# Far-score work placed by the length of VectorE's queue, and fewer small VectorE operations, in a hybrid decoder layer

## The chip, the cores and the metric

One Trainium2 chip, one of its cores. The metric is the device time of one execution in microseconds (us), the median of several runs. TensorE multiplies matrices (PE in the profile, its weight loads PEld), VectorE (DVE), ScalarE (ACT) and GpSimd (POOL) work element by element, and SyncE (SP) issues nearly all DMAs from one queue.

## What is computed

One layer for a prompt of 512 tokens and for 8 samples of 4 tokens each, 544 rows in all, in fp32. Between two gated feed-forward blocks stands a mixer: one input projection feeds dilated attention (8 heads of 64) and an mLSTM (4 heads of 128), side by side, and an output projection joins them.

```python
x = x + 0.5 * swiglu(rmsnorm(x), ffn1)
z = rmsnorm(x) @ w_in
# attention, per head: softmax over windows (128, 1), (512, 4), (2048, 16) of (window, dilation),
# the three merged by their softmax denominators; samples read a cache of 2048 keys and values
m = max(s); p = exp(s - m); den = sum(p); o = (p / den) @ v
# mLSTM, per head, in chunks of 128 tokens
d = where(causal, b[t] - b[s] + ig[s], -inf)
a = exp(d - m_t) * (q @ k.T)
num = a @ v + w_inter * (q @ C)
den = max(abs(sum(a) + w_inter * (q @ n)), exp(-m_t))
h = num / den
x = x + concat(attention, rmsnorm(h) * sigmoid(o_gate)) @ w_out
x = x + 0.5 * swiglu(rmsnorm(x), ffn2)
```

## The kernel before, in words

The activations lie transposed, 128 features by 544 rows to a tile. Every large product is made of three passes with operands split into a high and a low part (`whi`, `wlo` for weights; `xh`, `xl`, `mh`, `ml` and others for activations). ScalarE casts the high part and VectorE subtracts to get the low part (`Job.split`, L531). A job is one block of 128 output columns: 48 matmuls of 272 columns into the PSUM tile `mm` for a depth of 1024. The jobs run in a fixed order: feed-forward 1; the input projection (q, keys and values of the attention, then for each of the four mLSTM heads k, v, q and the output gate); the output projection in two passes (`wo`, L1780: first three mLSTM heads, then the four attention parts and the last mLSTM head); feed-forward 2.

The order of all other work is written while the program is built. The class `Order` (L54) keeps a modelled clock for each engine (`od.clock`) and a time `od.t` that goes with TensorE. The parts of the mixer are generators. Each yields the modelled time from which it wants to go on, and between the matmuls of the jobs `poll` (L100) lets every generator go on whose time has come. What it issues then takes the next place in its engine's queue. On the chip the queues are in order: an instruction that waits holds up what stands behind it on its engine.

The generators that the change touches:

- `far_scores` (L1136): for 8 samples and 6 blocks of cached keys, 48 times, it loads a key tile `kv` (and for each sample a broadcast query tile `qb`) by DMA, multiplies them on GpSimd into `pr` (128x512), and sums `pr` over 64 columns on VectorE into a slice of `big["sF"]`, which the profile calls `cb`, the tile that holds it. A product was placed when GpSimd's modelled clock was at most 1.5 us ahead, a sum when VectorE's was (`SCORE_AHEAD`, L45, L1163, L1168).
- `attn_pair` (L1350): prompt attention of two heads for one block of 128 queries. VectorE adds the mask to the scores and takes the row maxima `smax` (128x1 each, together 128x2), multiplies them by -0.125 (L1364), ScalarE takes the exponential with them as its bias, VectorE takes the reciprocal of the sums `sden`, ScalarE scales, TensorE transposes `pS` into `pT` and multiplies by the values. This runs 16 times.
- `ml_head` (L1590): one mLSTM head. VectorE adds a column of `cols` and the causal mask (part of the tile `ca`) to the row `E`, chunk by chunk; ScalarE exponentiates `E` whole; VectorE multiplies it with the products of q and k into `aT` (and `aTs` for the samples). `post` (L1649) forms the denominators `dn` with three small operations and a reciprocal, three times a head. GpSimd makes `qw`, `qm`, copies of the state's normaliser, and products with `hN` and `hf`.

The consumers of the far scores are `sample_soft` (L1410) and `sample_att` (L1455), for two groups of four samples. A group starts when its far scores are complete. Then 28 value tiles of the cache (`kv` from `cache_v_win`) are loaded and multiplied by TensorE; the second group's loads follow the last far score. The result feeds the second pass of the output projection. `reload` (L485) brings the eight tiles `x` back from DRAM for `wo`, by the same SP queue, and `E`, `W` and the state tiles `C` of each mLSTM head are loaded by it too.

Of the kernel before, what the change touches and what calls it, by code (L numbers as in the profile page):

```python
# [41 lines left out]
HB = B // 2  # L42
KS = float(P) ** -0.5
NT2 = 62
SCORE_AHEAD = 1.5  # L45
SCORE_PRIO = 1
SWITCH = 0.093
SLACK = 0.8
# [5 lines left out]
class Order:  # L54
# [89 lines left out]
    def R(self, *aps):  # L144
        return max(self.ready.get(a.tensor.name, (0.0, ""))[0] for a in aps) + 0.2
# [103 lines left out]
def hybrid_layer_kernel(ctx: ExitStack, tc: tile.TileContext, I: dict, C: dict, O: list):  # L249
# [23 lines left out]
    def bc(ap, axis, n):  # L273
        a = ap.unsqueeze(axis)
        shape = list(a.shape)
        shape[axis] = n
        return a.broadcast_to(shape)
# [858 lines left out]
    def far_scores():  # L1136
# [22 lines left out]
        for n, (b, i) in enumerate(order):  # L1159
            if n + 2 < len(order):  # L1160
                yield from fetch(*order[n + 2])
            k, q = ks[(b, i)], qs[b]
            yield max(R(k, q) - 0.3, od.clock["pool"] - SCORE_AHEAD)  # L1163
            pr = t2("pr", (P, ROW))
            pool.tensor_tensor(pr, k, q, op=OP.mult)
            pend.append((b, i, pr))
            if len(pend) > 1:
                yield max(R(pend[0][2]) - 0.3, od.clock["dve"] - SCORE_AHEAD)  # L1168
                reduce(*pend.pop(0))
            if n + 1 == len(order) // 2:  # L1170
                yield R(pend[0][2]) - 0.3
                reduce(*pend.pop(0))
                ev.add(("far", 0))
# [176 lines left out]
    def attn_pair(j, po, qbs):  # L1350
        for qb in qbs:
# [9 lines left out]
            for e, p in enumerate(ps2):  # L1361
                dve.tensor_tensor_reduce(out=s2[e][:, 0:w], in0=p[:, 0:w], in1=big["maskA"][:, (3 - qb) * P:], scale=1.0,
                                         scalar=-3.0e38, op0=OP.add, op1=OP.max, accum_out=mx[:, e:e + 1])
            dve.tensor_scalar(mx, mx, -0.125, None, op0=OP.mult)  # L1364
            done(*ps2)
            yield R(mx) - 0.4
            for e in range(2):
                act.activation(s2[e][:, 0:w], s2[e][:, 0:w], AF.Exp, bias=mx[:, e:e + 1], scale=0.125,
                               accum_out=dn[:, e:e + 1])
# [220 lines left out]
    def ml_head(h):  # L1590
# [7 lines left out]
            dma.dma_start(c0[:, :, 0:P], I["state_C"][i * HB:(i + 1) * HB, h].rearrange("b k v -> k b v"))  # L1598
        yield R(E, W) - 0.3, 0, lambda: "kws" in d and "vs" in d
        q, k, kw, kws, vm, vs, vb = (d[x] for x in ("q", "k", "kw", "kws", "vm", "vs", "vb"))  # L1600
        for c in range(CH):
            s_ = slice(c * P, (c + 1) * P)
            dve.scalar_tensor_tensor(E[:, s_], E[:, s_], cols[:, c, 0, h:h + 1], big["caus"], op0=OP.add, op1=OP.add)
        dve.scalar_tensor_tensor(E[0:NS, S:N], E[0:NS, S:N], cols[0:NS, CH, 0, h:h + 1], causS, op0=OP.add, op1=OP.add)
        qw = t2("qw")
        pool.tensor_tensor(qw, q, W, op=OP.mult)
        for i, c0 in enumerate(C0):
            pool.tensor_copy(c0[:, :, P], n0[:, i * HB:(i + 1) * HB, h])
        yield R(E) - 0.3
        act.activation(E[:, 0:S], E[:, 0:S], AF.Exp)  # L1610
        act.activation(E[0:NS, S:N], E[0:NS, S:N], AF.Exp)
        yield R(E) - 0.8, 2
        p, p2 = aux(), aux()
        for c in range(CH):
# [34 lines left out]
        def post(c0, nch, p, n, out):  # L1649
            dn, sq = small("dn", (P, 2), 4), small("sqj", (P, P), 2)  # L1650
            r = dn[0:n, 0:nch]
            dd = p[0:n, 0:nch * V1].rearrange("p (e v) -> p e v", v=V1)[:, :, P]
            dve.tensor_scalar(r, dd, -1.0, None, op0=OP.mult)
            dve.tensor_tensor(r, r, dd, op=OP.max)
            dve.tensor_tensor(r, r, cols[0:n, c0:c0 + nch, 2, h], op=OP.max)
            dve.reciprocal(r, r)
            yield R(dn) - 0.3
            for e in range(nch):
                act.activation(out(c0 + e), p[0:n, e * V1:e * V1 + P], AF.Copy, scale=dn[0:n, e:e + 1])
            done(p)  # L1660
            yield R(out(c0 + nch - 1)) - 0.3
            for e in range(nch):
                act.activation(sq[0:n], out(c0 + e), AF.Square, accum_out=ss[0:n, c0 + e:c0 + e + 1])
            posted.append(c0)
# [268 lines left out]
```

## Time and profile before

| | |
|---|---|
| time, three runs | 1125.67 us median (1123.56 to 1129.19) |
| the profiled execution's own time | 1125.39 us |
| its span, first to last instruction | 1123.2 us |
| TensorE busy | 1100.7 us (98%) |
| VectorE busy | 768.5 us (68%), 1228 instructions |
| ScalarE busy | 507.8 us (45%) |
| GpSimd busy | 92.5 us (8%) |
| granted TensorE clock, mean | 0.998 |
| HBM read, written | 132.57 MB, 9.18 MB |

The mixer runs from about 400 to 710 us of the span. GpSimd works in little else: its 48 products `pr` start between 475.3 and 595.5 us. Busy TensorE means that some matmul is in flight; matmuls overlap, so a busy share of 98% is not a rate of 98%.

### The profile page before, as it was taken

How to read it: one execution, taken by the hardware profiler on the slowest of the kernel's cores; microseconds unless marked ns; L12 is line 12 of the kernel's file. 1: busy time of each engine (PE TensorE's matmuls, PEld its weight loads, DVE VectorE, ACT ScalarE, POOL GpSimd, SP SyncE). 2: the span in 40 equal slices, each digit the busy share in tenths (PEclk: the TensorE clock that was granted, in tenths of full speed). 3: DMA queues.
4: the chain of work that ended last, by engine and by line, in shares of the span. 5: the costliest groups of instructions: out<-in, count | busy, mean ns of one | idle time of the engine just before them, and what ended most of it. 6: DMA issues, size and time to landing. Idle time of an engine off the chain costs nothing.

```text
span 1123.2 us, 21366 instructions
## 1 busy us (share of the span) xinstructions
PE 1100.7 (98%) x8807; PEld 1046.1 (93%) x8807; DVE 768.5 (68%) x1228; ACT 507.8 (45%) x905; POOL 92.5 (8%) x104
## 2 busy tenths in 40 slices
PE   7999999999999999999999999999999999999998
PEld 5999999999999989987887869999999999999998
DVE  5888337883487679689795737778962687537752
ACT  5545215551255465455564634454541355314541
POOL 0000000000000000066461201000000000000000
PEclk9999999999999999999999999999999999999999
DMA  7214312442133555576899285342242122422232
GB/s 232 82 36 143 123 38 76 132 133 75 39 126 113 165 161 150 189 216 191 259 283 309 69 278 171 106 144 76 75 138 89 60 91 76 151 76 76 67 105 60
DMA packets 143372, 145.36 MB, mean 129 GB/s; under 512 B 9012, under 2 KB 120916, under 8 KB 143276
## 3 DMA queue, kind: packets, MB, share of 16 engines
q1 hardware_dynamic: 143212, 144.01, 41.3%
q8 instruction: 69, 1.13, 0.4%
q14 instruction: 27, 0.22, 0.1%
q0 software_dynamic: 64, 0.00, 0.0%
HBM read 132.57 MB, written 9.18 MB: 126 GB/s over the span
## 4 chain that ended last, share of the span: by engine, by line
PE 80%; DVE 11%; DMA 4%; ACT 3%; issue 2%; SPq 1%; POOL 0%; DVEq 0%; ACTq 0%; POOLq 0%
PE mm L289 66%; PE aux L289 10%; PE aux L295 3%; DVE wlo L227 3%; ACT whi L227 2%; DVE ws L227 1%; DMA qb<-q_d 1%; DMA wraw<-in_ffn_w_up_dram 1%; DVE wraw L227 1%; SPq L227 1%; DVE cb L227 1%; DMA kv<-in_cache_k_win_dram 1%; DMA xt<-in_x_prompt_dram 0%; DMA wraw<-in_w_in_dram 0%; DVE mo L227 0%
## 5 line engine op out<-in xcount | busy, mean ns | idle before, releaser
L227 ACT CAST whi<-wraw 128x1024 fp32r<-128x1024 f32 (+3 forms) x180 | 174.1, 987 | 121.1 <-PE mm L289 91.3
L227 DVE TENSOR_TENSOR wlo<-wraw,whi 128x1024 fp32r<-128x1024 f32 (+3 forms) x180 | 207.3, 1160 | 23.6 <-ACT whi L227 23.3
L289 PE MATMUL mm<-oh,wlo 128*128 128x272 f32 x720 | 209.6, 291 | 2.2 <-DVE wlo L227 2.1
L289 PE MATMUL mm<-oh,whi 128*128 128x272 f32 x720 | 207.4, 288 | 0.0
L289 PE MATMUL mm<-ol,whi 128*128 128x272 f32 x720 | 207.1, 288 | 0.0
L289 PE MATMUL mm<-xh,whi 128*128 128x272 f32 x704 | 155.2, 302 | 0.2 <-ACT whi L227 0.2
L289 PE MATMUL mm<-hh,whi 128*128 128x272 f32 x704 | 147.2, 289 | 0.5 <-DVE x L227 0.5
L289 PE MATMUL mm<-xl,whi 128*128 128x272 f32 x704 | 146.5, 290 | 0.5 <-DVE xl L227 0.5
L289 PE MATMUL mm<-xh,wlo 128*128 128x272 f32 x704 | 146.5, 290 | 0.3 <-DVE wlo L227 0.3
L289 PE MATMUL mm<-hl,whi 128*128 128x272 f32 x704 | 146.5, 288 | 0.0
L289 PE MATMUL mm<-hh,wlo 128*128 128x272 f32 x704 | 146.4, 288 | 0.0
L227 DVE SCALAR_TENSOR_TENSOR x<-mm,x 128x544 f32<-128x544 f32 (+1 forms) x49 | 34.9, 713 | 154.8 <-PE mm L289 154.8
L289 PEld LDWEIGHTS mm<-oh,wlo 128*128 128x128 f32 x720 | 135.4, 188 | 5.5 <-DVE wlo L227 4.4
L289 PEld LDWEIGHTS mm<-ol,whi 128*128 128x128 f32 x720 | 135.6, 188 | 0.0
L289 PEld LDWEIGHTS mm<-oh,whi 128*128 128x128 f32 x720 | 135.6, 188 | 0.0
L289 PEld LDWEIGHTS mm<-xh,whi 128*128 128x128 f32 x704 | 110.2, 190 | 14.2 <-issue 13.0
L289 PEld LDWEIGHTS mm<-xl,whi 128*128 128x128 f32 x704 | 111.3, 190 | 0.7 <-DVE xl L227 0.7
L289 PEld LDWEIGHTS mm<-xh,wlo 128*128 128x128 f32 x704 | 111.3, 190 | 0.6 <-DVE wlo L227 0.6
L289 PEld LDWEIGHTS mm<-hh,whi 128*128 128x128 f32 x704 | 110.8, 188 | 0.9 <-DVE x L227 0.8
L289 PEld LDWEIGHTS mm<-hh,wlo 128*128 128x128 f32 x704 | 110.9, 188 | 0.0
L289 PEld LDWEIGHTS mm<-hl,whi 128*128 128x128 f32 x704 | 110.7, 188 | 0.0
L227 ACT CAST whi<-ws 128x1024 fp32r<-128x1024 f32 x54 | 56.7, 1050 | 103.1 <-DVE ws L227 103.0
(328 smaller groups left out, 1777.5 us busy)
## 6 DMA issues: line engine op xcount, KB each, us to landing
wraw<-in_ffn_w_gate_dram SPq DMA_DIRECT2D x40, 512.0 KB
wraw<-in_ffn_w_up_dram SPq DMA_DIRECT2D x36, 512.0 KB
wraw<-in_ffn_w_down_dram SPq DMA_DIRECT2D x16, 1024.0 KB
kv<-in_cache_k_win_dram SPq DMA_DIRECT2D x56, 256.0 KB
kv<-in_cache_v_win_dram SPq DMA_DIRECT2D x56, 256.0 KB
wraw<-in_w_in_dram SPq DMA_DIRECT2D x16, 512.0 KB
wraw<-in_ffn_w_down_dram SPq DMA_DIRECT2D x8, 768.0 KB
wraw<-in_w_in_dram SPq DMA_DIRECT2D x6, 1024.0 KB
```

The lines of the kernel that those rows point to most:

```text
L227: r = fn(*args, **kw)
L289: nc.tensor.matmul(out, lhsT, rhs, start=start, stop=stop, **kw)
L295: nc.tensor.transpose(out, in_, idn)
```

## The change

The far-score products and sums are placed when VectorE's modelled queue reaches at most 0.8 us past the present time; the sums no longer look 1.5 us ahead. Three sets of small VectorE operations are made fewer. The maxima are multiplied by -0.125 on ScalarE. The column of `cols` becomes the bias of the exponential on ScalarE, one exponential for each chunk, and VectorE adds only the mask, one operation of 128x512 in place of four of 128x128. The lower bound of the denominator goes into the operation that negates it.

```diff
-SCORE_AHEAD = 1.5
...
             k, q = ks[(b, i)], qs[b]
-            yield max(R(k, q) - 0.3, od.clock["pool"] - SCORE_AHEAD)
+            yield max(R(k, q) - 0.3, od.clock["pool"] - 0.2)
+            while od.clock["dve"] - od.t > 0.8:
+                yield od.clock["dve"] - 0.8
             pr = t2("pr", (P, ROW))
             pool.tensor_tensor(pr, k, q, op=OP.mult)
             pend.append((b, i, pr))
             if len(pend) > 1:
-                yield max(R(pend[0][2]) - 0.3, od.clock["dve"] - SCORE_AHEAD)
+                yield R(pend[0][2]) - 0.3
+                while od.clock["dve"] - od.t > 0.8:
+                    yield od.clock["dve"] - 0.8
                 reduce(*pend.pop(0))
...
-            dve.tensor_scalar(mx, mx, -0.125, None, op0=OP.mult)
             done(*ps2)
             yield R(mx) - 0.4
+            act.activation(mx, mx, AF.Copy, scale=-0.125)
...
-        for c in range(CH):
-            s_ = slice(c * P, (c + 1) * P)
-            dve.scalar_tensor_tensor(E[:, s_], E[:, s_], cols[:, c, 0, h:h + 1], big["caus"], op0=OP.add, op1=OP.add)
-        dve.scalar_tensor_tensor(E[0:NS, S:N], E[0:NS, S:N], cols[0:NS, CH, 0, h:h + 1], causS, op0=OP.add, op1=OP.add)
+        E4 = E[:, 0:S].rearrange("p (c n) -> p c n", c=CH)
+        dve.tensor_tensor(E4, E4, bc(big["caus"], 1, CH), op=OP.add)
+        dve.tensor_tensor(E[0:NS, S:N], E[0:NS, S:N], causS, op=OP.add)
...
-        act.activation(E[:, 0:S], E[:, 0:S], AF.Exp)
-        act.activation(E[0:NS, S:N], E[0:NS, S:N], AF.Exp)
+        for c in range(CH):
+            s_ = slice(c * P, (c + 1) * P)
+            act.activation(E[:, s_], E[:, s_], AF.Exp, bias=cols[:, c, 0, h:h + 1])
+        act.activation(E[0:NS, S:N], E[0:NS, S:N], AF.Exp, bias=cols[0:NS, CH, 0, h:h + 1])
...
-            dve.tensor_scalar(r, dd, -1.0, None, op0=OP.mult)
+            dve.scalar_tensor_tensor(r, dd, -1.0, cols[0:n, c0:c0 + nch, 2, h], op0=OP.mult, op1=OP.max)
             dve.tensor_tensor(r, r, dd, op=OP.max)
-            dve.tensor_tensor(r, r, cols[0:n, c0:c0 + nch, 2, h], op=OP.max)
             dve.reciprocal(r, r)
```

Since the places depend on the modelled clocks, the whole mixer's order shifts with it. Three places are shown as the built programs have them (rows of the changed kernel carry L226 for L227, since one line above is gone; x8 is eight instructions alike in a row).

GpSimd, around the second mLSTM head (`qw` to `nP` are that head's own work, `vm` and `vs` belong to the next head's v job). Before:

```order
L227 MEMSET vs 128x1
L227 TENSOR_TENSOR pr<-kv,qb 128x512 x8
L227 TENSOR_TENSOR qw<-mq,W 128x544
L227 COPY C_6723<-n_123 128x4
L227 COPY C_6724<-n_123 128x4
L227 TENSOR_TENSOR pr<-kv,qb 128x512 x9
L227 TENSOR_TENSOR qm<-qw,ca 128x64
L227 COPY nP<-Cst 128x1
L227 MEMSET vm 128x4
```

GpSimd at the same place, now:

```order
L226 TENSOR_TENSOR pr<-kv,qb 128x512 x5
L226 TENSOR_TENSOR qw<-mq,W 128x544
L226 COPY C_6668<-n_123 128x4
L226 COPY C_6669<-n_123 128x4
L226 TENSOR_TENSOR pr<-kv,qb 128x512 x5
L226 TENSOR_TENSOR qm<-qw,ca 128x64
L226 TENSOR_TENSOR pr<-kv,qb 128x512
L226 COPY nP<-Cst 128x1
L226 TENSOR_TENSOR pr<-kv,qb 128x512 x3
L226 MEMSET vm 128x4
L226 MEMSET vs 128x1
L226 TENSOR_TENSOR pr<-kv,qb 128x512 x4
```

Before, the 9 products ahead of `qm` are the last of the 48. Now 16 products stand behind that `qm`: 8 of them in the rows shown, 8 more later, the last two right behind the `nP` of the third head.

VectorE, the twelve instructions up to `aTs` of the first mLSTM head, with tile numbers. Before:

```order
L227 TENSOR_SCALAR smax_5563<-smax_5563 128x2
L227 SCALAR_TENSOR_TENSOR E_5478<-E_5478,cols_126,ca_4014 128x128 x4
L227 SCALAR_TENSOR_TENSOR E_5478<-E_5478,cols_126,c_causS_112 32x32
L227 TENSOR_REDUCE cb_4015<-pr_5530 128x8
L227 COPY pT_5612<-aux_5601 128x512
L227 TENSOR_REDUCE cb_4015<-pr_5589 128x8
L227 RECIPROCAL sden_5564<-sden_5564 128x2
L227 TENSOR_TENSOR mo_5622<-mm_5486,rb_4440 128x544
L227 TENSOR_REDUCE cb_4015<-pr_5616 128x8
L227 TENSOR_TENSOR wlo_5626<-wraw_5140,whi_5625 128x1024
L227 TENSOR_TENSOR aT_5664<-aux_5657,E_5478 128x512
L227 TENSOR_TENSOR aTs_5665<-aux_5658,E_5478 32x32
```

VectorE at the same place, now:

```order
L226 RECIPROCAL sden_5477<-sden_5477 128x2
L226 TENSOR_TENSOR E_5488<-E_5488,ca_4014 128x512
L226 TENSOR_TENSOR E_5488<-E_5488,c_causS_112 32x32
L226 TENSOR_REDUCE cb_4015<-pr_5506 128x8
L226 RECIPROCAL sden_5519<-sden_5519 128x2
L226 TENSOR_REDUCE cb_4015<-pr_5572 128x8
L226 TENSOR_TENSOR mo_5600<-mm_5496,rb_4440 128x544
L226 COPY pT_5622<-aux_5612 128x512
L226 COPY pT_5624<-aux_5613 128x512
L226 TENSOR_REDUCE cb_4015<-pr_5595 128x8
L226 TENSOR_TENSOR aT_5651<-aux_5644,E_5488 128x512
L226 TENSOR_TENSOR aTs_5652<-aux_5645,E_5488 32x32
```

The low part of a weight tile (`wlo`, 128x1024) no longer stands right ahead of `aT`, but before the rows shown and again two rows behind `aTs`. The scaling of `smax` is gone, and `E` takes two instructions in place of five.

SP's queue, from the second group's value tiles on. Before (all 24 tiles that follow the group's first four, then the loads for the fourth mLSTM head and for the output projection):

```order
L227 DMA kv<-in_cache_v_win_dram 128x512 x8
L227 DMA kv<-in_cache_v_win_dram 128x1x512 x12
L227 DMA kv<-in_cache_v_win_dram 128x512 x4
L227 DMA out_dram<-C_7428 128x4x128
L227 DMA out_dram<-C_7429 128x4x128
L227 DMA E<-uw_d 128x544
L227 DMA W<-uw_d 128x544
L227 DMA C_8173<-in_state_C_dram 128x4x128
L227 DMA C_8174<-in_state_C_dram 128x4x128
L227 DMA x<-x_d 128x544 x3
L227 DMA wraw<-in_w_out_dram 128x3x256
L227 DMA x<-x_d 128x544 x5
```

SP's queue at the same place, now:

```order
L226 DMA kv<-in_cache_v_win_dram 128x512 x8
L226 DMA out_dram<-C_7334 128x4x128
L226 DMA E<-uw_d 128x544
L226 DMA W<-uw_d 128x544
L226 DMA C_8058<-in_state_C_dram 128x4x128
L226 DMA C_8059<-in_state_C_dram 128x4x128
L226 DMA x<-x_d 128x544
L226 DMA kv<-in_cache_v_win_dram 128x1x512 x4
L226 DMA x<-x_d 128x544
L226 DMA wraw<-in_w_out_dram 128x3x256
L226 DMA x<-x_d 128x544
L226 DMA kv<-in_cache_v_win_dram 128x1x512 x4
```

Of the 24 value tiles, 16 now stand behind the loads of `E`, `W` and `C` and among those of `x`: 8 in the rows shown, 8 more among and behind the last five `x`.

## The prediction, made before the changed kernel ran

> **What bounds the kernel now.** I read the page first, then the windows of the mixer, then TensorE's waits in the window where it is not busy throughout, then the timelines around the longest wait.
>
> The page's busy times and the chain that ended last, by engine:
>
> ```profile
> PE 1100.7 (98%) x8807; PEld 1046.1 (93%) x8807; DVE 768.5 (68%) x1228; ACT 507.8 (45%) x905; POOL 92.5 (8%) x104
> ...
> PE 80%; DVE 11%; DMA 4%; ACT 3%; issue 2%; SPq 1%; POOL 0%; DVEq 0%; ACTq 0%; POOLq 0%
> ```
>
> TensorE sets the time, and the change takes no matmul away. So all that can be won is time in which TensorE waits or runs slowly, and only where the order changes. The windows (us of the span, the length, then the busy time of each engine, the clock, the DMA share, GB/s):
>
> ```profile
> 476.00:600.00 124.00, 118.83 (x983) 101.78 (x985) 110.79 (x228) 66.71 (x163) 74.91 (x65) 0.99 0.79 239
> 600.00:710.00 110.00, 110.00 (x974) 89.01 (x967) 63.58 (x191) 52.28 (x150) 13.90 (x26) 1.00 0.63 204
> ```
>
> From 476 to 600 TensorE is idle for 124.00 - 118.83 = 5.2 us, VectorE is busy for 89% and GpSimd for 60%. From 600 to 710 TensorE is never idle, VectorE is busy for 58%. TensorE's waits in the first window (total, times, longest):
>
> ```profile
> PE aux L295 <- ACT pS L227: 1.4, 1, 1.4
> PE aux L295 <- DVE aTs L227: 1.0, 1, 1.0
> PE aux L295 <- DVE smax L227: 0.8, 2, 0.5
> PE aux L295 <- DMA kv<-in_cache_k_win_dram: 0.7, 1, 0.7
> PE aux L295 <- DVE C L227: 0.6, 1, 0.6
> PE aux L289 <- DVE ml L227: 0.3, 1, 0.3
> PE aux L289 <- DVE Cst L227: 0.2, 1, 0.2
> PE aux L289 <- DVE pT L227: 0.2, 1, 0.2
> ```
>
> Nine waits, 5.2 us, all but one behind VectorE, or behind ScalarE that waited for VectorE. TensorE around the longest:
>
> ```profile
> 514.92 0.41 PE L289 MATMUL mm<-xl,whi 128*128 128x272 f32 x2
> 515.16 0.42 PE L289 MATMUL mm<-xh,wlo 128*128 128x272 f32 x2
> 516.95 0.33 PE L295 MATMUL aux<-ident,pS 128*128 128x128 f32 x1 [1.37 <-ACT pS L227]
> ...
> 518.18 0.66 PE L289 MATMUL mm<-xl,whi 128*128 128x272 f32 x2
> 518.63 0.66 PE L289 MATMUL mm<-xh,wlo 128*128 128x272 f32 x2
> ```
>
> A pair of matmuls begins every 0.25 us but is listed with 0.41, so each wait hides another 0.16 us: 9 x 0.16 = 1.4. Behind this wait a pair takes 518.63 - 518.18 = 0.45 us, and two windows show why:
>
> ```profile
> 516.00:520.00 4.00, 2.80 (x13) 2.64 (x14) 3.44 (x11) 2.97 (x10) 0.75 (x1) 0.70 0.64 234
> 520.00:524.00 4.00, 3.84 (x23) 2.58 (x22) 4.00 (x10) 2.42 (x7) 1.77 (x2) 0.87 0.40 85
> ```
>
> The granted clock falls to 0.70 and 0.87. The 12 matmuls there cost 6 x (0.45 - 0.25) = 1.2 us. So the pot is 5.2 + 1.4 + 1.2 = 7.8 us, of which the wait for a key tile (0.7 + 0.16 = 0.9) is none of the change's. I take 6.9 us as what VectorE's lateness costs.
>
> Why VectorE is late stands just ahead of that wait (GpSimd, then VectorE):
>
> ```profile
> 511.54 4.26 POOL L227 TENSOR_TENSOR pr<-kv,qb 128x512 f32<-128x512 f32 x3 [4.42 <-DMA kv<-in_cache_k_win_dram]
> ...
> 511.66 1.18 DVE L227 TENSOR_TENSOR dn<-dn,cols 128x1 f32<-128x1 f32 x1
> ...
> 513.05 1.61 DVE L227 TENSOR_TENSOR rr<-rr,sg 128x544 f32<-128x544 f32 x1
> ```
>
> An operation on one column takes 1.18 us while a product `pr` runs. The minimum, median and maximum over the kernel show who suffers this:
>
> ```profile
> L227 DVE TENSOR_TENSOR dn<-dn,cols x12: 159/161/1178, 509.8 to 691.7; 128x2 f32<-128x2 f32 x8, 128x1 f32<-128x1 f32 x4
> L227 DVE TENSOR_SCALAR smax<-smax x16: 169/171/1080, 468.3 to 663.2; 128x2 f32<-128x2 f32 x16
> L227 DVE SCALAR_TENSOR_TENSOR E<-E,cols,ca x16: 328/341/1487, 488.0 to 682.1; 128x128 f32<-128x128 f32 x16
> L227 DVE TENSOR_REDUCE cb<-pr x48: 656/674/686, 476.6 to 597.6; 128x8 f32<-128x512 f32 x48
> L227 POOL TENSOR_TENSOR pr<-kv,qb x48: 1266/1293/2193, 475.3 to 595.5; 128x512 f32<-128x512 f32 x48
> ```
>
> The first three sometimes lose about one product's time (1.29 us); the sums never do. The change removes the first two or moves them to ScalarE, and cuts the third from four instructions to one.
>
> [...]
>
> **The change part by part.** VectorE's groups in the window 476 to 600 (busy us, mean ns), with the nearest rows for what replaces them (`aT`, `aTs`, and three on ScalarE):
>
> ```profile
> L227 DVE TENSOR_SCALAR smax<-smax 128x2 f32<-128x2 f32 x10 | 4.9, 485 | 0.3
> L227 DVE SCALAR_TENSOR_TENSOR E<-E,cols,ca 128x128 f32<-128x128 f32 x8 | 4.7, 644 | 0.0
> L227 DVE SCALAR_TENSOR_TENSOR E<-E,cols,c_causS 32x32 f32<-32x32 f32 x2 | 1.5, 750 | 0.0
> L227 DVE TENSOR_TENSOR aT<-aux,E 128x512 f32<-128x512 f32 x2 | 1.4, 684 | 0.0
> L227 DVE TENSOR_TENSOR aTs<-aux,E 32x32 f32<-32x32 f32 x2 | 0.3, 169 | 0.0
> ...
> L227 ACT ACTIVATE pS<-pS,smax 128x128 f32<-128x128 f32 x8 | 3.1, 394 | 5.9 <-DVE smax L227 5.9
> L227 ACT ACTIVATE E<-E 128x512 f32<-128x512 f32 x4 | 2.5, 634 | 6.8 <-DVE E L227 6.8
> L227 ACT ACTIVATE E<-E 32x32 f32<-32x32 f32 x4 | 0.9, 218 | 0.6 <-DVE E L227 0.6
> ```
>
> - Maxima: 4.9 us leave VectorE. ScalarE gets ten more instructions of about 0.2 us (by the 218 row), each where it would have waited for VectorE anyway. Behind them in ScalarE's queue stand the exponential that needs them and the next weight cast. ScalarE is busy for 66.71 of 124, so I cost this at nothing; without that cover it is 0.2 us for each of 16 chains.
> - `E`: 4.7 + 1.5 = 6.2 us become 2 x (0.68 + 0.17) = 1.7 by the rows of `aT` and `aTs`, or 4.3 if each 128x512 add meets a product. I take the low end, since two exposed instructions stand for ten: 4.5 us saved. ScalarE pays 4 x 0.39 - 0.63 = 0.9 us more a head. The head's chain gets no longer: five adds and one exponential, 4 x 0.34 + 0.23 + 0.63 = 2.2 undisturbed and up to 1.3 more for each collision, become 0.68 + 0.17 + 4 x 0.39 = 2.4.
> - `dn`: 12 instructions fewer, 6 in this window, 5 x 0.16 + 1.18 = 2.0 us.
> - Far scores: 16 products and sums move past the second head's `qm`, where all had been done: 16 x 0.674 = 10.8 us leave the window. Their 16 key tiles move with them on SP's queue, 16 x 256 KB, and find the DMAs idle:
>
> ```profile
> 620.00:648.00 28.00, 28.00 (x252) 24.99 (x253) 19.09 (x51) 16.98 (x43) 6.14 (x9) 1.00 0.17 53
> ```
>
> VectorE's load in the first window falls by 4.9 + 4.5 + 2.0 + 10.8 = 22 us, from 110.8 to about 89 of 124 (72%). The second window gets 10.8 and loses a few, about 70 of 110 (64%), and 16 chances of a collision. Both lie well under the 89% at which TensorE waits today. The collisions left fall on `wlo`, `rr`, `mo` and the like. I let a third of VectorE's waits stay: these are 5.2 + 1.4 - 0.9 = 5.7 us, so 3.8 go. The clock's 1.2 us go with the wait ahead of them.
>
> [...]
>
> The price is the later end. The second group's values now come while `E`, `W`, `C` and `x` are loaded, and some matmul may wait for them; its bounds stand under the third rival. In the forecast I put 0.5 us, near the nearest row of such a wait (0.7 for a key tile).
>
> The sum is 3.8 + 1.2 - 0.5 = 4.5 us off the profiled execution's 1125.39 (span 1123.2), so **1120.9 us**. That execution lies 0.3 under the median of the runs, 1125.67. A measurement can tell about 0.5%, 5.6 us: faster means under 1120.0, slower above 1131.3.
>
> **The rivals.**
>
> First, all of it comes back: 6.9 us and no new wait, 1118.5. For it: at 72% few queues build up on VectorE. Against it: the products are no shorter and fewer than half leave the window. If the key tile's wait goes too, 1117.6.
>
> Second, the collisions stay. A product placed when VectorE's queue is short still takes 1.29 us; the queue was at most 0.8 us, so whatever comes next finds the product running and loses up to 1.29 us. Then only what the removed operations caused comes back: the waits behind `smax` (0.8 + 0.3) and the 1.0 us that the `dn` row lost ahead of the longest wait, 2.1 us: 1123.3. For it: `rr` takes 1.61 us in the row above with products still running, and the change leaves `rr` alone. Against it: the sums leave the window as well. [...]
>
> Third, slower: the second group's values come late. The rows of today's last two stretches, of two short windows inside them, and of the loads themselves on SP:
>
> ```profile
> 652.00:656.00 4.00, 4.00 (x52) 2.94 (x50) 1.79 (x6) 1.83 (x9) 0.00 (x0) 1.00 1.03 371
> 668.00:696.00 28.00, 28.00 (x248) 24.34 (x248) 18.01 (x50) 11.02 (x32) 4.61 (x7) 1.00 0.63 183
> 672.00:676.00 4.00, 4.00 (x44) 2.53 (x36) 1.44 (x2) 1.44 (x3) 0.10 (x1) 1.00 1.02 206
> ...
> 647.82 16.58 SPq L227 DMA_DIRECT2D kv<-in_cache_v_win_dram  x24
> ```
>
> From 668 to 696 the DMAs are free for 37% of 28 us, 10.4 us. The changed order puts 16 value tiles behind the loads that run there, 16 x 0.262 = 4.2 MB. At 371 GB/s, as value tiles run today, that is 11.3 us, 0.9 more than is free. At 206, as with `E`, `W` and `C` under way, it is 20.4 us, 10 too many. Then TensorE, in order, waits in the output projection: 1125.39 - 5.0 + 10.0 = 1130.4; 1 us more, if an output of `C` ahead of these tiles waits for VectorE, makes it 1131.4. It decides from about 270 GB/s down, where the loads take 5.0 us more than is free (4.2 MB in 15.4 us) and the gain is gone. Against it: the queue can run ahead of TensorE, as SP does in the row above.
>
> **How the numbers follow.** The forecast gets 0.38 with a range of its own of 1119 to 1123; the first rival 0.22, the second 0.23, the third 0.17. Under 1120.0 lie the first rival and a third of the forecast's chance, 0.22 + 0.13 = 0.35. Above 1131.3 lie those cases of the third in which SP's queue is held up as well, 0.12. The rest, 0.53, is no change that can be told. The range reaches from a full gain with the key tile's wait gone and 1 us for the runs' spread, 1116.5, to 1129.0, which leaves out most of the third rival.
>
> **What would show it.** In the changed kernel's profile VectorE should be busy for about 72% between 476 and 600 and 64% between 600 and 705. TensorE's idle time there should fall from 5.2 to about 2 us, and the clock should stay at 1.00. The wait of `pS` for ScalarE at 1.4 us should be gone. The sums should end near 650 in place of 598, and matmuls that read value tiles should show waits of under 1 us. I am wrong if TensorE waits for `kv` in the output projection (third rival), if `rr`, `mo` and `wlo` still take a product's time and TensorE's waits remain (second), or if new waits appear before 476 or behind 710, where I expect none.

## The result, and the profile after

The changed kernel takes 1118.85 us (median of 12 runs, 1117.62 to 1120.66), the kernel before on the same chip 1125.16 us (12 runs, 1122.64 to 1129.19). The ratio is 0.9947, 95% interval 0.9937 to 0.9957: 6.3 us faster, where 4.5 were forecast. The profiled execution took 1117.62 us, the fastest of the 12; its span is 1115.6.

The page's busy times and its chain by engine:

```profile
PE 1098.4 (98%) x8807; PEld 1044.2 (94%) x8807; DVE 750.1 (67%) x1186; ACT 512.5 (46%) x935; POOL 92.0 (8%) x104
...
PE 87%; DVE 7%; ACT 3%; DMA 2%; issue 1%; SPq 0%; DVEq 0%; ACTq 0%
```

TensorE has 7 points more of the chain, VectorE and the DMAs have lost 6 together. The two windows of the mixer, same columns as in the prediction:

```profile
476.00:600.00 124.00, 124.00 (x1075) 105.69 (x1073) 92.74 (x210) 74.59 (x201) 62.64 (x58) 1.00 0.77 234
600.00:710.00 110.00, 110.00 (x936) 90.62 (x933) 67.75 (x177) 51.79 (x147) 25.07 (x33) 1.00 0.66 212
```

TensorE's idle time from 476 to 600 has gone from 5.2 us to nothing, and the clock is 1.00. VectorE is busy for 92.74 / 124 = 75% and 67.75 / 110 = 62%, where 72% and 64% were forecast. All that TensorE waits for between 300 us and the end is listed in four rows. They stood in the kernel before with the same numbers, and none of these waits lies between 400 and 710 us:

```profile
PE aux L288 <- DVE wlo L226: 1.7, 4, 1.0
PE mm L288 <- DVE wlo L226: 0.8, 4, 0.2
PE aux L294 <- DVE x L226: 0.6, 1, 0.6
PE mm L288 <- DVE x L226: 0.5, 1, 0.5
```

The new and the moved operations, one row for each tile (minimum, median, maximum in ns):

```profile
L226 ACT ACTIVATE smax<-smax x16: 186/204/219, 468.3 to 647.1; 128x2 f32<-128x2 f32 x16
L226 DVE TENSOR_TENSOR E<-E,ca x4: 680/688/1595, 485.7 to 662.1; 128x512 f32<-128x512 f32 x4
L226 DVE SCALAR_TENSOR_TENSOR dn<-aux,cols x12: 140/156/160, 504.4 to 675.1; 128x2 f32<-128x2 f32 x8, 128x1 f32<-128x1 f32 x4
L226 DVE TENSOR_REDUCE cb<-pr x48: 657/675/689, 476.0 to 636.3; 128x8 f32<-128x512 f32 x48
L226 POOL TENSOR_TENSOR pr<-kv,qb x48: 1267/1291/2350, 474.7 to 632.7; 128x512 f32<-128x512 f32 x48
```

The lengths are those that the prediction took: 0.2 us on ScalarE, 0.69 for the mask, 0.16 for `dn`. One of the four mask instructions took 1.60 us, at 613.98; GpSimd ran `qw` then, not a product. The sums end at 636, not near 650. In VectorE's groups of the first window 38 of the 48 sums still stand (instructions, busy us, mean ns, idle before):

```profile
L226 DVE TENSOR_REDUCE cb<-pr 128x8 f32<-128x512 f32 x38 | 25.3, 675 | 7.4 <-POOL pr L226 7.3
L226 DVE TENSOR_TENSOR wlo<-wraw,whi 128x1024 fp32r<-128x1024 f32 x12 | 16.8, 1403 | 0.6 <-ACT whi L226 0.4
```

So 10 left, where I had 16, and that is the 92.74 in place of 89: 6 x 0.675 = 4 us. The second row, to be read beside that of the kernel before, says something else:

```profile
L227 DVE TENSOR_TENSOR wlo<-wraw,whi 128x1024 fp32r<-128x1024 f32 x11 | 15.9, 1446 | 0.6 <-ACT whi L227 0.6
```

`wlo` alone takes 1.22 us, the median over the changed kernel. Its mean in the window is 1.40 us after and was 1.45 before. On `wlo` the collisions with the products have hardly become fewer, and yet TensorE no longer waits. On other operations they have become fewer. I counted in the traces the VectorE operations that ran beside a product and took at least 0.1 us longer than the shortest tenth of their kind (same tiles and shape). In the kernel before there are 27, which lose about 19 us in all; in the changed kernel there are 11, which lose about 7 us. `rr`, which the prediction names under the second rival, shows it (before, then after):

```profile
L227 DVE TENSOR_TENSOR rr<-rr,sg x8: 702/708/1606, 415.6 to 526.3; 128x544 f32<-128x544 f32 x8
L226 DVE TENSOR_TENSOR rr<-rr,sg x8: 704/713/868, 414.7 to 519.5; 128x544 f32<-128x544 f32 x8
```

One price is to be seen. In the changed kernel a group of eight matmuls on value tiles, 1.06 us elsewhere, takes 1.81 us, and the list of the weight loads' waits has its cause:

```profile
668.54 1.81 PE L288 MATMUL aux<-kv,pTA 128*32 128x512 f32 x8
```

```profile
PEld aux L288 <- DMA kv<-in_cache_v_win_dram: 0.5, 1, 0.5
```

Six of the group's weight loads start from 668.54 on; the last two, at 669.30, have waited 0.53 us for a value tile. Matmuls of the same group are in flight meanwhile, so TensorE counts as busy: this wait is in no row of its idle time.

**Where 6.6 us went in the profiles.** The profiled spans can't be compared to the microsecond, since the 101st `mm` matmul starts anywhere between 33.0 and 36.3 us in kernels whose beginning is the same. So I count from the 2,901st to the 4,301st `mm` matmul (454.6 to 744.8 us before), with the same 2,404 matmuls between them in every kernel. That stretch lasts 290.3 us before and 283.7 after. Three things were summed from the traces: TensorE's idle time, the time from start to start of the 112 matmuls on value tiles, and half the length of each spell, that is of each time in which the granted clock was 0.50. What is left of the stretch is 269.5 before and 269.1 after, so these three hold nearly all of the difference: -5.2 idle, -1.7 clock (a spell of 3.41 us), +0.7 value tiles, -0.5 the rest. The same count over all kernels of this study, with VectorE's busy time from 476 to 600 us (the rows of it that matter are quoted below):

| kernel | median us | ratio to before, 95% interval | VectorE busy | TensorE idle | value matmuls | half clock | stretch | the rest |
|---|---|---|---|---|---|---|---|---|
| before | 1125.16 | 1 | 110.8 | 5.2 | 13.9 | 3.4 | 290.3 | 269.5 |
| after | 1118.85 | 0.9947 (0.9937 to 0.9957) | 92.7 | 0.0 | 14.6 | 0 | 283.7 | 269.1 |
| e1_place | 1121.59 | 0.9976 (0.9962 to 0.9990) | 100.4 | 0.7 | 16.2 | 0 | 286.2 | 269.4 |
| e2_small | 1132.55 | 1.0072 (1.0049 to 1.0094) | 98.5 | 8.2 | 15.6 | 10.2 | 298.7 | 269.8 |
| e2b_ahead14 | 1122.65 | 0.9983 (0.9971 to 0.9995) | 102.0 | 5.3 | 13.8 | 0 | 288.4 | 269.3 |
| c16_before | 1124.30 | 1.0000 (0.9988 to 1.0012) | 109.2 | 6.6 | 13.9 | 0 | 290.0 | 269.6 |
| e3_no_far | 1117.58 | 0.9933 (0.9913 to 0.9952) | 69.2 | 0.0 | 14.1 | 0 | 281.8 | 267.7 |
| e4_on_dve | 1130.04 | 1.0055 (1.0034 to 1.0075) | 103.4 | 7.5 | 13.9 | 6.8 | 294.8 | 270.0 |
| u_smax | 1119.94 | 0.9958 (0.9944 to 0.9972) | 101.3 | 1.5 | 13.9 | 0 | 284.7 | 269.3 |
| u_E | 1117.74 | 0.9942 (0.9929 to 0.9955) | 96.9 | 0.8 | 13.9 | 0 | 283.1 | 268.4 |
| u_dn | 1118.07 | 0.9934 (0.9916 to 0.9953) | 93.1 | 0.0 | 13.9 | 0 | 283.1 | 269.2 |
| sum_rule | 1121.15 | 0.9965 (0.9952 to 0.9979) | 93.9 | 2.4 | 16.1 | 0 | 288.1 | 269.7 |
| limit_15 | 1120.06 | 0.9956 (0.9941 to 0.9971) | 96.3 | 0.2 | 14.9 | 0 | 284.0 | 268.9 |
| limit_06 | 1119.09 | 0.9941 (0.9920 to 0.9961) | 91.8 | 0.2 | 14.0 | 0 | 283.4 | 269.2 |

The ratio is to the kernel before on the same chip as the experiment, whose median was 1124.02, 1124.22 and 1124.95 us for the three sets of four. A profile is one execution, and a median is of several: the profiled executions lie from 2.0 us under their kernel's median (e3_no_far) to 3.4 us over it (e2b_ahead14). The stretch leaves out the start, where e2b_ahead14 is already 2.0 us behind the kernel before (36.3 against 34.3 us at the 101st matmul).

### The profile page after: what moved, and what is told of

It reads as the page before. It is cut to its first block, busy times and chain, and to the rows that moved or that the text cites. A ratio compares the mean times of both kernels' runs of the same rounds, so it can differ in the third digit from the quotient of the medians.

```text
span 1115.6 us, 21347 instructions
## 1 busy us (share of the span) xinstructions
PE 1098.4 (98%) x8807; PEld 1044.2 (94%) x8807; DVE 750.1 (67%) x1186; ACT 512.5 (46%) x935; POOL 92.0 (8%) x104
## 4 chain that ended last, share of the span: by engine, by line
PE 87%; DVE 7%; ACT 3%; DMA 2%; issue 1%; SPq 0%; DVEq 0%; ACTq 0%
PE mm L288 71%; PE aux L288 12%; PE aux L294 4%; DVE wlo L226 3%; ACT whi L226 2%; DVE ws L226 1%; DMA wraw<-in_ffn_w_up_dram 1%; DVE wraw L226 1%; DMA xt<-in_x_prompt_dram 0%; DVE zu L226 0%; DVE ol L226 0%; ACT p L226 0%; DVE xd L226 0%; SPq L226 0%; DVE hl L226 0%
## 5 line engine op out<-in xcount | busy, mean ns | idle before, releaser
L226 ACT CAST whi<-wraw 128x1024 fp32r<-128x1024 f32 (+3 forms) x180 | 174.1, 988 | 120.7 <-PE mm L288 91.0
L226 DVE TENSOR_TENSOR wlo<-wraw,whi 128x1024 fp32r<-128x1024 f32 (+3 forms) x180 | 207.1, 1159 | 23.9 <-ACT whi L226 23.6
L226 DVE SCALAR_TENSOR_TENSOR x<-mm,x 128x544 f32<-128x544 f32 (+1 forms) x49 | 35.0, 714 | 154.9 <-PE mm L288 154.9
L288 PEld LDWEIGHTS mm<-hh,whi 128*128 128x128 f32 x704 | 110.8, 188 | 0.9 <-DVE x L226 0.8
L288 PEld LDWEIGHTS mm<-xl,whi 128*128 128x128 f32 x704 | 110.8, 189 | 0.8 <-DVE xl L226 0.8
L288 PEld LDWEIGHTS mm<-xh,wlo 128*128 128x128 f32 x704 | 110.8, 189 | 0.6 <-DVE wlo L226 0.6
L226 ACT CAST whi<-ws 128x1024 fp32r<-128x1024 f32 x54 | 56.7, 1051 | 104.0 <-DVE ws L226 103.9
```

The costliest lines, as they stand in the source:

```text
L226: r = fn(*args, **kw)
L288: nc.tensor.matmul(out, lhsT, rhs, start=start, stop=stop, **kw)
```

## The experiments

The theory: TensorE's waits in the mixer are VectorE's lateness, and both parts of the change bring some of it back. The rivals put it down to one part alone, or to the order that each new plan happens to give. The letters A, B and C of the first four expectations (e1 to e4) are not those of the other eight, which c16_before and u_dn explain.

### The two parts apart

**Placement alone (e1_place).** The kernel before with the new conditions for products and sums, all small operations as before.

```diff
-            yield max(R(k, q) - 0.3, od.clock["pool"] - SCORE_AHEAD)
+            yield max(R(k, q) - 0.3, od.clock["pool"] - 0.2)
+            while od.clock["dve"] - od.t > 0.8:
+                yield od.clock["dve"] - 0.8
...
-                yield max(R(pend[0][2]) - 0.3, od.clock["dve"] - SCORE_AHEAD)
+                yield R(pend[0][2]) - 0.3
+                while od.clock["dve"] - od.t > 0.8:
+                    yield od.clock["dve"] - 0.8
```

> The placement of products and sums alone; smax, E and dn as before the change. Theory A (TensorE waits behind VectorE because of its load and of collisions with GpSimd's products; both parts of the change relieve it): a half to two thirds of the gain, 1120.5 to 1122.5 us, TensorE idle 1 to 3 us between 476 and 600. Theory B (placement alone did it, the small operations are hidden): all of it, 1118 to 1119.5. Theory C (the small operations alone did it): 1124 or more.

Measured: 1121.59 us, ratio 0.9976 (0.9962 to 0.9990), in the range that Theory A gave, and with less idle time than the 1 to 3 us that it gave. Its first window and what its matmuls and weight loads waited for:

```profile
476.00:600.00 124.00, 123.33 (x1071) 106.29 (x1069) 100.41 (x230) 69.82 (x179) 63.57 (x58) 1.00 0.78 233
```

```profile
PE aux L289 <- DVE pT L227: 0.7, 1, 0.7
```

```profile
PEld aux L289 <- DMA kv<-in_cache_v_win_dram: 1.7, 4, 0.5
```

TensorE's idle time falls from 5.2 to 0.7 us by the placement alone, the clock's spell is gone, and the median improves by 2.4 only. Part of the difference is in the last row: value tiles come late four times, and their matmuls take 16.2 us in place of 13.9.

**The small operations alone (e2_small).** The change's edits of `mx`, `E` and `dn` on the kernel before, with the lead for products and sums at 1.6 us in place of 1.5.

```diff
-SCORE_AHEAD = 1.5
+SCORE_AHEAD = 1.6
...
-            dve.tensor_scalar(mx, mx, -0.125, None, op0=OP.mult)
+            act.activation(mx, mx, AF.Copy, scale=-0.125)
...
-            dve.scalar_tensor_tensor(E[:, s_], E[:, s_], cols[:, c, 0, h:h + 1], big["caus"], op0=OP.add, op1=OP.add)
+        dve.tensor_tensor(E4, E4, bc(big["caus"], 1, CH), op=OP.add)
...
-            dve.tensor_scalar(r, dd, -1.0, None, op0=OP.mult)
+            dve.scalar_tensor_tensor(r, dd, -1.0, cols[0:n, c0:c0 + nch, 2, h], op0=OP.mult, op1=OP.max)
...
```

> The small operations alone; products and sums placed up to 1.6 us ahead, close to the 1.5 of before. Theory A: 1121 to 1123 us, VectorE's collisions on wlo, rr and mo still there. Theory B: 1124.5 or more. Theory C: 1118 to 1119.5.

Measured: 1132.55 us, ratio 1.0072 (1.0049 to 1.0094), slower than the kernel before. Theory B's "1124.5 or more" holds the number, but no theory gave a reason for a loss. The loss has its place. From 684 to 700 us TensorE waits four times at the end of the mixer's last head:

```profile
PE mm L289 <- DVE ml L227: 1.8, 1, 1.8
PE aux L289 <- ACT hN L227: 1.2, 2, 0.6
PE mm L289 <- ACT mh L227: 0.9, 1, 0.9
```

And the clock falls there for 10.2 us (the slice ahead of the spell, then the first two of the spell's three):

```profile
686.30:689.70 3.40, 2.71 (x17) 1.72 (x14) 3.10 (x15) 2.40 (x10) 1.41 (x3) 1.00 0.23 65
689.70:693.10 3.40, 2.48 (x10) 1.43 (x8) 2.31 (x5) 1.95 (x7) 2.38 (x3) 0.50 0.32 96
693.10:696.60 3.50, 1.75 (x8) 1.76 (x9) 3.17 (x11) 0.00 (x0) 0.75 (x2) 0.50 0.26 77
```

No such wait stands at this place in the kernel before or after. Two things were new, the small operations and the lead, so two controls followed.

**The lead alone (c16_before).** `SCORE_AHEAD = 1.6` in the kernel before, nothing else.

> The kernel before with its own lead for products and sums at 1.6 in place of 1.5, the value that the kernel with the small operations alone had; nothing else. It is the control for that kernel's 1132.55 us. Theory A (the small operations do take work off VectorE; the 1132.55 us came of the order in which the mixer's last heads then stood, 5.1 us of TensorE's waits and 10.24 us at half clock between 685 and 700 us): this lead may move the order as well; any time from 1121 to 1131 us fits, and with the waits of the end of the mixer it would be over 1127. Theory B (the small operations cost time by themselves: the exponential in five pieces and the scale on ScalarE make each head's chain longer): within 2 us of the kernel before, 1123 to 1127 us. Theory C (each new plan of the order moves the time by several us whatever is in it): off from the kernel before by over 2 us, up or down.

Measured: 1124.30 us, ratio 1.0000 (0.9988 to 1.0012). Theories A and B both allowed this. The lead itself is worth nothing.

**The small operations with another lead (e2b_ahead14).** As e2_small, with `SCORE_AHEAD = 1.4`.

> The small operations alone once more, with the lead at 1.4 in place of 1.6. Theory A: without the waits at 685 to 700 us 1120 to 1124 us; some of the waits at 490 to 550 us stay, since 48 products and sums still stand between 475 and 600 us. Theory B: 1130 to 1135 us again. Theory C: anywhere from 1118 to 1132 us, with the waits at other places.

Measured: 1122.65 us, ratio 0.9983 (0.9971 to 0.9995), within Theory A's 1120 to 1124 us. So it wasn't the small operations either that cost 8 us in e2_small, but the order that they and that lead gave together. What in the plan led to it was not tried. The first window and TensorE's waits of e2b_ahead14:

```profile
476.00:600.00 124.00, 118.81 (x997) 102.91 (x996) 102.04 (x209) 69.14 (x178) 74.34 (x65) 1.00 0.80 242
```

```profile
PE aux L295 <- DVE smax L227: 2.1, 2, 1.6
PE aux L295 <- DVE C L227: 1.4, 1, 1.4
PE aux L289 <- DVE aT L227: 1.1, 1, 1.1
PE aux L295 <- DVE kw L227: 0.5, 1, 0.5
```

This is the row to lay beside that of e1_place. VectorE is busy for 102.0 us here and for 100.4 there, all but the same. TensorE is idle for 5.2 us in this window here, as much as in the kernel before, and for 0.7 there. By their times the two kernels are not apart, since their intervals overlap and e1_place pays 2.3 us on value tiles. Their waits are apart, though each is read from one execution.

So VectorE's load alone does not decide whether TensorE waits. The other kernels agree: e2_small is idle for 4.2 us in this window at a load of 98.5 us, sum_rule (below) for 2.4 at 93.9, and the kernels with both conditions for 0 to 1.2 at 92 to 103. Among these last the idle time does grow with the load, so the load has a part. The collisions don't tell the two kernels apart either, about 12 us here and 11 in e1_place by the count above.

What differs is what stands in VectorE's queue ahead of the operation that TensorE needs. In all five waits of e2b_ahead14 a sum stands right ahead of that operation or one operation further ahead. The first of them (VectorE, then TensorE):

```profile
498.61 0.67 DVE L227 TENSOR_REDUCE cb<-pr 128x8 f32<-128x512 f32 x1
499.20 0.68 DVE L227 TENSOR_TENSOR aT<-aux,E 128x512 f32<-128x512 f32 x1
...
499.94 0.71 PE L289 MATMUL aux<-vm,kw 128*128 128x129 f32 x4 [1.09 <-DVE aT L227]
```

Counted from the traces, stretches of over 6 us in which VectorE has no break of over 0.1 us take up 101 of the 124 us before, 83 in e2b_ahead14, 42 in e1_place and 41 in the changed kernel; 47 of the 48 sums start in this window in e2b_ahead14 and 37 in e1_place. The placement changes that; the small operations take 9 us off VectorE and leave most of it. The count isn't all of it either: sum_rule, with 39 us of such stretches, still has its 2.4 us of waits.

### How much there was to win

**No far-score work (e3_no_far).** The kernel before without the products and sums; the far scores are set to zero once.

```diff
+        pool.memset(big["sF"], 0.0)
...
-            pr = t2("pr", (P, ROW))
-            pool.tensor_tensor(pr, k, q, op=OP.mult)
+            pr = k
...
-            dve.tensor_reduce(big["sF"][:, b // 4, i, b % 4], pr.rearrange("p (h d) -> p h d", h=NH), axis=AX.X,
-                              op=OP.add)
+            pass
```

> The kernel before with the 48 products and sums of the far scores left out (their loads stay, the scores are set to zero once). Theory A: without their 31.7 us on VectorE and without collisions TensorE's waits go, 1117.5 to 1119.5 us, not below the changed kernel by more than 1 us. If the order of TensorE's work or the loads were the cause (theory D), the waits would stay in part and it would come out at 1121 or more.

Measured: 1117.58 us, ratio 0.9933 (0.9913 to 0.9952). Its first window has no idle TensorE and a VectorE at 56%:

```profile
476.00:600.00 124.00, 124.00 (x1068) 103.38 (x1066) 69.21 (x199) 66.70 (x171) 9.05 (x20) 1.00 0.89 279
```

The changed kernel, which computes the far scores, comes within the intervals of the kernel that leaves them out, 0.9947 against 0.9933. These runs can't tell that there is more to win from this work.

### VectorE loaded again

**The products on VectorE (e4_on_dve).** The changed kernel with the 48 products on VectorE, and the limit on its queue at 1.0 in place of 0.8.

```diff
-            while od.clock["dve"] - od.t > 0.8:
-                yield od.clock["dve"] - 0.8
+            while od.clock["dve"] - od.t > 1.0:
+                yield od.clock["dve"] - 1.0
...
-            pool.tensor_tensor(pr, k, q, op=OP.mult)
+            dve.tensor_tensor(pr, k, q, op=OP.mult)
...
```

> The changed kernel with the 48 products on VectorE in place of GpSimd (queue limit 1.0 us in place of 0.8): 48 x 0.69 = 33 us more work on VectorE, and no product on GpSimd to collide with. [...] If the load is the cause, VectorE is busy for about 86% between 476 and 600 and waits return: 1122 to 1128.

Measured: 1130.04 us, ratio 1.0055 (1.0034 to 1.0075), above what was expected, and not for the reason that was meant. In the first window TensorE is idle for 1.2 us only, at 103.4 us of VectorE. The loss is one wait behind it, for `C`:

```profile
PE aux L288 <- DVE C L226: 5.8, 1, 5.8
```

The timelines of SyncE and of VectorE show why `C` was late:

```profile
617.98 1.77 SPq L226 DMA_DIRECT2D kv<-in_cache_v_win_dram  x4
621.52 0.55 SPq L226 DMA_DIRECT2D kv<-in_cache_k_win_dram  x1
...
625.86 0.69 DVE L226 TENSOR_TENSOR pr<-kv,qb 128x512 f32<-128x512 f32 x1 [6.60 <-DMA out_dram<-C]
626.47 1.12 DVE L226 SCALAR_TENSOR_TENSOR C<-C,W,aux 128x129 f32<-128x129 f32 x4
```

The product, now in VectorE's queue, waits 6.6 us for its key tile, which SyncE issued at 621.52 behind four value tiles, and `C` stands behind the product. (The row names an output of `C` as what ended the wait. That output is issued next on the same queue; the product reads only `kv` and `qb`, so I take the key tile's landing for the cause.) In the changed kernel GpSimd's products wait for key tiles as well, seven times between 476 and 710 us:

```profile
POOL pr L226 <- DMA kv<-in_cache_k_win_dram: 16.1, 7, 4.1
```

There these 16.1 us stand in GpSimd's queue, and TensorE has no wait in the mixer. So collisions with products aren't needed for TensorE to wait: e4_on_dve has no product on GpSimd, and TensorE is idle for 7.5 us. What 48 more operations on VectorE cost without the wait for the key tile stays open.

### The small operations one by one, and other limits

Each of the next three is the changed kernel with one edit undone.

**Maxima scaled on VectorE again (u_smax).**

```diff
+            dve.tensor_scalar(mx, mx, -0.125, None, op0=OP.mult)
...
-            act.activation(mx, mx, AF.Copy, scale=-0.125)
```

> The changed kernel with one edit undone: the scaling of the score maxima is a VectorE operation again. Theory A: 16 operations of 0.17 to 1.08 us come back on VectorE, some 3 to 6 us of its time; of it TensorE feels a part, 1119 to 1121 us. Theory B: not slower than the changed kernel, 1117 to 1119 us. Theory C: over 2 us off from 1118.85 us in either direction.

Measured: 1119.94 us, ratio 0.9958 (0.9944 to 0.9972).

**Decay in four pieces on VectorE again (u_E).**

```diff
-        dve.tensor_tensor(E4, E4, bc(big["caus"], 1, CH), op=OP.add)
+            dve.scalar_tensor_tensor(E[:, s_], E[:, s_], cols[:, c, 0, h:h + 1], big["caus"], op0=OP.add, op1=OP.add)
...
-            act.activation(E[:, s_], E[:, s_], AF.Exp, bias=cols[:, c, 0, h:h + 1])
+        act.activation(E[:, 0:S], E[:, 0:S], AF.Exp)
...
```

> The changed kernel with one edit undone: the decay's mask and its column are added in four 128-column operations on VectorE again, and the exponential is one operation on ScalarE. Theory A: 16 operations of 0.34 us and more for 4 of 0.68 us on VectorE, about 3 us of its time and its collisions; TensorE feels part of it, 1119 to 1121 us. Theory B: 1117 to 1119 us. Theory C: over 2 us off from 1118.85 us in either direction.

Measured: 1117.74 us, ratio 0.9942 (0.9929 to 0.9955).

**Denominator in three operations again (u_dn).**

```diff
-            dve.scalar_tensor_tensor(r, dd, -1.0, cols[0:n, c0:c0 + nch, 2, h], op0=OP.mult, op1=OP.max)
+            dve.tensor_scalar(r, dd, -1.0, None, op0=OP.mult)
             dve.tensor_tensor(r, r, dd, op=OP.max)
+            dve.tensor_tensor(r, r, cols[0:n, c0:c0 + nch, 2, h], op=OP.max)
```

> The changed kernel with one edit undone: the denominator is negated and compared in three VectorE operations again. Theory A (with the sums spread to the later jobs VectorE has room to spare, and any one small operation can come back at little cost): 16 operations of 0.16 us come back, 2.6 us of VectorE's time that TensorE hardly feels, 1118 to 1120 us. Theory B (the small operations count for their own length): 1120 to 1122 us. Theory C (every new order moves the time by several us): over 2 us off from 1118.85 us.

Measured: 1118.07 us, ratio 0.9934 (0.9916 to 0.9953). All three intervals overlap that of the changed kernel, 0.9937 to 0.9957. With the placement in, no single edit is worth anything that these runs can tell. u_E and u_dn lie under the changed kernel by their medians, but not by their intervals, so none of them is shown to be better. u_smax and u_dn fell in Theory A's ranges and u_E in Theory B's, which lie too close together to be told apart here.

**Only the sum waits for a short queue (sum_rule).** The product has its old condition.

```diff
+SCORE_AHEAD = 1.5
...
-            yield max(R(k, q) - 0.3, od.clock["pool"] - 0.2)
-            while od.clock["dve"] - od.t > 0.8:
-                yield od.clock["dve"] - 0.8
+            yield max(R(k, q) - 0.3, od.clock["pool"] - SCORE_AHEAD)
```

> The changed kernel in which only the sum waits for a short VectorE queue; the product has its old condition, a lead of 1.5 on GpSimd. Since at most two products are under way ahead of their sums, the sums are still spread, from 474 to about 630 us. Theory A: 1118 to 1120.5 us, with less than 1 us of TensorE's waits. Theory B as A. Theory C: over 2 us off from 1118.85 us.

Measured: 1121.15 us, ratio 0.9965 (0.9952 to 0.9979), slower than any theory but C had it. The rows of its sums, which end at 615 us and not near 630, of its first window and of its value tiles:

```profile
L227 DVE TENSOR_REDUCE cb<-pr x48: 653/676/687, 477.3 to 615.3; 128x8 f32<-128x512 f32 x48
```

```profile
476.00:600.00 124.00, 121.65 (x1042) 103.41 (x1041) 93.94 (x212) 72.00 (x195) 67.16 (x63) 1.00 0.80 244
```

```profile
PEld aux L289 <- DMA kv<-in_cache_v_win_dram: 1.9, 4, 0.6
```

VectorE has no more to do here than in the changed kernel, 93.9 against 92.7 us, and TensorE is idle for 2.4 us again. By the profile the condition on the product has its part. By the times that isn't shown: the intervals of the two kernels, 0.9952 to 0.9979 and 0.9937 to 0.9957, overlap.

**The limit at 1.5 and at 0.6 (limit_15, limit_06).** The changed kernel with another number in both places.

```diff
-            while od.clock["dve"] - od.t > 0.8:
-                yield od.clock["dve"] - 0.8
+            while od.clock["dve"] - od.t > 1.5:
+                yield od.clock["dve"] - 1.5
...
```

> The changed kernel with the limit on VectorE's queue at 1.5 in place of 0.8, for product and sum: the sums end earlier, near 615 us. Theory A: half-way between a dense and a spread placement, 0 to 2 us of TensorE's waits, 1118 to 1121.5 us. Theory C: over 2 us off from 1118.85 us in either direction, with waits that do not follow the limit.

> The changed kernel with the limit at 0.6: the sums are spread a little more, to about 640 us. Theory A: no waits of TensorE for VectorE, 1117.5 to 1120.5 us; the second group's values come later, and value tiles may hold TensorE for 0.5 to 1.7 us inside their groups of matmuls. Theory C: over 2 us off from 1118.85 us.

Measured: 1120.06 us, ratio 0.9956 (0.9941 to 0.9971), and 1119.09 us, 0.9941 (0.9920 to 0.9961). Both lie in Theory A's ranges, and TensorE's idle time is 0.2 us in both. Between 0.6 and 1.5 the number hardly matters. With both conditions in, five other orders (the three u kernels and these two) lie within 1.3 us of the changed kernel; the larger swings that Theory C asked for came where a condition was missing (sum_rule, e2_small) or where VectorE had the products as well (e4_on_dve).

## Why the prediction was right, point by point

- **The pot.** 5.2 us of idle TensorE went whole, the key tile's wait of 0.7 among it, which I had counted as none of the change's. The clock's term was 1.2 in the forecast and is 3.41 / 2 = 1.7 by the length of the spell. What each wait hides, 9 x 0.16 = 1.4, is not shown: the rest of the stretch fell by 0.5, and it differs by more than that between other kernels of the table. Together 7.4 us against 7.8.
- **"I let a third of VectorE's waits stay."** This is the step that failed, and its 1.9 us cover the difference between 4.5 and 6.3 us. None stayed. That the 5.7 us of which it was a third came out as 5.2 + 0.5 is in part luck: the 0.9 us of the key tile, which I had left out, and the 0.9 that the hidden part lacked cancel. I took VectorE's share as the measure, 89% at which TensorE waits and 72% at which some waits remain. e1_place and e2b_ahead14 speak against that measure: at 81% and 82% TensorE's idle time was 0.7 and 5.2 us. What went with the waits are VectorE's long stretches without a break, 42 us in e1_place and 83 in e2b_ahead14: the placement keeps the sums out of VectorE's queue where that is long.
- **The small operations.** Their lengths and the loads on both engines came as forecast, ScalarE's 0.2 us in 16 chains cost TensorE nothing. But I let them carry half of the fall in VectorE's load, and with it half of the gain. Alone they gave a ratio of 0.9983 (0.9971 to 0.9995), and with the placement none of the three is needed singly. That all three together are worth the 2.7 us between e1_place and the changed kernel is what the medians say. The profile of e1_place puts 1.5 us of that on value tiles and 0.7 on idle time, and value tiles come late in sum_rule too, which has the small operations. How much of the 2.7 us is theirs, and how much the order's, is not settled.
- **The clock.** The spell went with the waits in the profiled execution, as forecast. How long the clock is low differs between executions of one kernel: the granted clock was 0.996 to 1.000, 0.9984 in the mean, in the 23 executions of the kernel before beside sum_rule, and 0.998 to 1.000, 0.9996 in the mean, in the 12 of the changed kernel. That is about 0.0012 x 1120 = 1.3 us, an estimate near the forecast's 1.2. The profiled executions of e2b_ahead14 and c16_before have the waits and no spell, so the two aren't tied one to one. The last section has more on it.
- **The price, 0.5 us for value tiles.** It came: 0.7 us, at 668.54, inside a group of matmuls.
- **First rival (all comes back, 1118.5).** This is what happened, 1118.85, with the key tile's wait gone and the price paid. The forecast's own narrower range, 1119 to 1123, was missed by 0.15 us.
- **Second rival (the collisions stay, 1123.3).** Its premise held in part: `wlo` still lost 0.19 us on average, but `rr`, which the rival names, fell from 1606 to 868 ns at most, `mo` took up to 1696 ns (1683 before), and of the about 19 us that collisions took about 7 are left. Its conclusion did not hold, since no wait of TensorE came of those that are left. I put that down to the shorter queue behind them (41 us of long stretches in place of 101), which is argued and not shown wait by wait.
- **Third rival (the values late, 1130.4).** In the changed kernel the DMAs ran at 378 GB/s where the second group's tiles stood, not at the 206 from which this rival lived:

```profile
664.00:680.00 16.00, 16.00 (x141) 13.16 (x140) 8.41 (x24) 8.01 (x27) 3.20 (x6) 1.00 1.06 378
```

  The small form of it is real all the same, 0.5 us here, 1.7 in e1_place and 1.9 in sum_rule.
- **Places.** I expected no new waits before 476 or behind 710 us, and there are none.

## What to carry to other kernels

When an engine off the critical path makes the bound engine wait, ask what stands in its queue ahead of the instruction that is waited for, and not only how busy it is: two kernels with VectorE at 81% and 82% had 0.7 and 5.2 us of waits. Filler work with operands that come late belongs on a queue behind which nothing urgent stands, and into other queues only when they are short: in e4_on_dve a product's 6.6 us of waiting in VectorE's queue cost TensorE a wait of 5.8 us, in the changed kernel 16.1 us of such waits in GpSimd's queue cost it none. And a change that re-plans an order needs a control with another value of the planner's number: one order of the same operations was 8 us slower than before, another 2 us faster.

## What the runs showed of the hardware

The clock at half speed (granted 0.50) came and went in spells of 3.41 us before, 6.83 in e4_on_dve and 10.24 in e2_small, that is once, twice and three times 3.41. By the traces' clock records each of these began a whole number of such lengths, to within 0.02, ahead of the spell at the end of its execution: 177 before, 147 in e4_on_dve, 129 in e2_small. Ahead of the first slow slice TensorE was not always idle. It was in e4_on_dve, where the second row is the slow slice that follows:

```profile
622.30:625.80 3.50, 0.00 (x0) 0.00 (x0) 0.00 (x0) 0.00 (x0) 0.00 (x0) 0.99 0.61 162
625.80:629.20 3.40, 1.98 (x9) 2.01 (x10) 3.34 (x8) 0.97 (x2) 1.48 (x2) 0.50 0.18 54
```

In the kernel before it was busy for 1.80 of 3.42 us in the slice ahead:

```profile
514.18:517.60 3.42, 1.80 (x15) 1.42 (x13) 3.39 (x7) 0.98 (x4) 1.62 (x1) 1.00 1.08 338
517.60:521.00 3.40, 3.24 (x14) 2.92 (x15) 2.84 (x11) 2.99 (x7) 1.75 (x2) 0.50 0.29 105
```

And in e2_small it was busy for 2.71 of 3.40 us (quoted above). But e2b_ahead14 has a slice with 1.82 of 3.40 us busy, and no spell follows:

```profile
535.40:538.80 3.40, 1.82 (x15) 1.59 (x15) 3.40 (x7) 0.76 (x3) 1.66 (x2) 1.00 0.97 328
```

So the clock fell behind a slice without a matmul in e4_on_dve and behind slices in which TensorE was busy for 53% (before) and 80% (e2_small), and not behind one of 54% in e2b_ahead14. Which slices are followed by a spell, these runs don't settle: the busy time alone does not tell it.
